# Where TensorE's operands lie in a partition: one place for all streamed tiles of a two-block model

## The chip, the cores and the metric

The kernel runs on one core of a Trainium2 chip. The metric is the device time of one execution in microseconds. A partition of SBUF is addressed in bytes; "place" below means an address in the partition modulo 256.

## The reference, cut to what matters

A token matrix `x` (256 tokens, 1,024 features, float32) goes through two layers of a first block and one layer of a second.

```python
for l in range(2):
    x = x + 0.5 * swiglu(rms_norm(x), gate, up, down)        # 1024 -> 2816 -> 1024
    proj = rms_norm(x) @ w_in                                 # 1024 -> 2944
    x = x + concat(rwkv7(proj), dilated_attention(proj), conv(proj)) @ w_out
    x = x + 0.5 * swiglu(rms_norm(x), gate, up, down)
h  = modulate(rms_norm(x));  hc = modulate(rms_norm(ctx))
ya, ys, yc = window_attention(h, hc), ssm(h, hc), grid_attention(h, hc)
x = x + gate1 * ((ga * (ya @ w_oa) + gb * (ys @ w_ob) + gc * (yc @ w_oc)) @ w_out)
h2 = modulate(rms_norm(x))
x = x + gate2 * ((silu(dwconv(h2 @ w_gate)) * (h2 @ w_up)) @ w_down)
return rms_norm(x) * final_norm
```

## The kernel before

Features lie on partitions, tokens along the partition, so a dense layer is a sum of products of 128 by 128 weight tiles (the stationary operand) with 128 by 256 activation tiles (the moving operand). To keep float32 accuracy every factor is split into a high part, rounded to the type `fp32r`, and a low part, the rest. `dense` then does three matmuls for one weight tile: high weights with high activations, low weights with high activations, high weights with low activations. Each matmul carries its own weight load, which runs beside the matmul before it.

Weights stream from HBM in chunks of eight tiles (`load_chunk`): SyncE's queue loads `wraw`, ScalarE writes `whi` (line 288 is the helper `act`), VectorE writes `wlo` (line 264 is the helper `tt`, line 283 `stt`), three buffers of each. All matmuls are recorded under line 291 (`mm`), transposes under line 295. The names of the stages in the trace are: `gu` gate and up projections of a feed-forward, `dn` its down projection, `win` the input projection of a first-block layer, `woa` and `wob` the two parts of its output projection, `c` and `p` the projections of context and tokens in the second block, `oa`, `ob`, `oc` the three branch projections, `o` the product with `w_out` in the second block (and, 64 rows of it, attention). The scheduler of the tile framework orders instructions on each engine by its own model of time; pinned instructions keep the program's order.

Activation tiles live in these tiles of SBUF:

- `xm`, a ring of 18 slots from `xt()`: the split `x` of every `gu`, `win`, `p` stage, and the inputs of `ob`, `o` and of the last feed-forward.
- `bigA`, `bigB` (6,144 columns each): the split hidden activations of a feed-forward (22 tiles of 256), the moving operands of `dn`; between feed-forwards they are working space.
- `F`: the split context, moving operand of `c`.
- `mixr` and `xr`, one ring: moving operands of `wob`, `oa` and `oc`.
- `E`, one working arena of 10,944 columns, from which `E(offset, shape)` cuts pieces.

The last feed-forward (`ffn_conv`) is different in two ways: its moving tile has 258 columns (two columns carry the shift), and in its down projection `down` the activations are the stationary operand (128 columns of `hh` or `hl`) while the weights move (512 columns of `whi` or `wlo`, 264 matmuls).

Tiles follow each other in the order of their first allocation, each rounded up to 32 bytes. Worked out from the tile sizes:

| tile | place before | place after |
|---|---|---|
| `whi`, `wlo` (every 128-column weight slice) | 32 | 32 |
| `xm` slots | 32, 64, 96, ... (1,056 bytes apart, all eight multiples of 32) | 224 (1,024 bytes apart) |
| `bigA`, `bigB` | 96 | 224 |
| `E`, or `Ea` and `Eb` | 96 | 224 |
| `F` | 128 | 224 |
| `mixr`, `xr` | 224 | 224 |

The distance of a moving operand behind the weights (its place less the weights' place, modulo 256) is therefore before: 64 in `dn`, 96 in `c`, 192 in `wob`, `oa` and `oc`, and any multiple of 32 in the stages that read `xm`. In the last down projection, with the roles changed (weights move, activations are stationary), it is 192 before.

Of the kernel before, what the change touches and what calls it, by code (L numbers as in the profile page):

```python
# [12 lines left out]
F32R = mybir.dt.float32r  # L13
# [7 lines left out]
P = 128  # L21
TOK = 256
# [4 lines left out]
XM = 18  # L27
XR = 8
BIG = 6144
EXT = 10944  # L30
FXT = 4096
# [177 lines left out]
class Ker:  # L209
# [16 lines left out]

    def arena(self, n, tag="E"):

        t = self.t([P, n], tag)

        def piece(off, *shape):
            m = 1
            for z in shape:
                m *= z
            a = t[:, off:off + m]
            if len(shape) == 1:
                return a
            nm = " ".join(f"d{i}" for i in range(len(shape)))
            return a.rearrange(f"p ({nm}) -> p {nm}", **{f"d{i}": z for i, z in enumerate(shape) if i})
        return piece  # L240

    def pin(self, ins):
        return self.tc.keep_in_program_order(ins)

    def xt(self, n=TOK):
        return self.t([P, TOK + 2], "xm", bufs=XM, dt=F32R)[:, 0:n]

# [223 lines left out]
    def setup(self):  # L471
# [30 lines left out]
        self.act(self.ones_r, t0.to_broadcast([P, P]), AF.Identity, bias=1.0)  # L502
        self.norm_begin()
        self.xs = [self.prep(k, g0[:, k:k + 1], False) for k in range(KD)]
        with self.first(-LATE):
# [3 lines left out]
    def load_b(self, name, parts, extra=None):  # L509
        idx, a = _cat(parts)  # L510
        t = self.t([P, 2180], "cb")
        n = a.shape[1]
        self.pin(self.nc.sync.dma_start(out=t[:, :n], in_=self.A[name]))
        if extra:
            idx["lora"] = (n, n + 384)
            self.pin(self.nc.sync.dma_start(out=t[:, n:n + 384], in_=self.A[extra]))
        return lambda k: t[:, idx[k][0]:idx[k][1]]
# [13 lines left out]
    def ffn(self, l, w, nxt):  # L531
# [3 lines left out]
        hh = self.t([P, BIG], "bigA", dt=F32R)  # L535
        hl = self.t([P, BIG], "bigB", dt=F32R)
        E = self.arena(EXT)
        mods = self.mod_part(E, 2 * l + w - 1)
# [40 lines left out]
    def mixer1(self, l, nxt):  # L579
        nc = self.nc  # L580
        col = lambda k, a=0, n=1: self.col(f"{k}.{l}", a, n)
        cb = self.load_b("cb1", _const_b1(), f"lora{l}")
        xs = self.xs
        R1, R2, E, F = self.arena(BIG, "bigA"), self.arena(BIG, "bigB"), self.arena(EXT), self.arena(FXT, "F")
        pb = R2(0, 10, TOK + 2)
        nc.gpsimd.memset(pb[:, :, 0:1], 0.0)
        mum = self.t([P, 10], "mum")
        self.ts(mum, col("shift_mu", 0, 10), -1.0, 1.0)
        att = E(8640, 9, TOK)
        cu = E(6016, 4, TOK)  # L590
        ps_sh = [R2(2600, 3, TOK), R1(0, 3, TOK), E(1536, 3, TOK)]
# [396 lines left out]
    def conv(self, l, cb, col, cu, E):  # L988
        nc = self.nc
        W = 30 + TOK  # L990
        z = E(7040, 2, W)
        nc.gpsimd.memset(z[:, :, 0:30], 0.0)
        th = E(7616, 2, TOK)
        self.act(th, cu[:, 2:4, :], AF.Tanh, scale=0.5)
        self.stt(z[:, :, 30:W], th, 1.0, cu[:, 0:2, :], ALU.add, ALU.mult)
        wh = self.t([P, 62], "cwh")
        self.ts(wh, col("conv_dw_w", 0, 62), 0.5, None)
        o = E(8128, 2, TOK)
        yield

        for j in range(31):
            for i in range(2):
                a, w = z[:, i, j:j + TOK], wh[:, i * 31 + j:i * 31 + j + 1]
# [9 lines left out]
        for i in range(2):  # L1013
            self.stt(o[:, i, :], ps[:, 0:TOK], -1.0 / 256, o[:, i, :])
        sq = E(7616, 2, TOK)
        self.act(sq, o, AF.Square)
# [202 lines left out]
    def ctx_path(self):  # L1219
        nc = self.nc  # L1220
        E, xs, R1 = self.E2, self.cxs, self.R1
# [5 lines left out]
        self.ts(self.cwh[:, 36:48], self.col("ssm_conv_b_2", 0, 12), 0.5, None)  # L1227
        pre = E(5120, 10, TOK + 2)
        nc.gpsimd.memset(pre[:, :, 0:1], 0.0)
# [87 lines left out]
    def block2(self):  # L1317
# [108 lines left out]
        self.norm_begin()  # L1426
        ys = []
        for i in range(KD):
            ps = self.pa("yT")
# [4 lines left out]
            self.norm_add(v)  # L1434
            hi = self.xt()
            lo = self.xt()
            g = self.col("ssm_norm_2", i)
# [11 lines left out]
        for n in range(KD):  # L1449
# [12 lines left out]
            ms.append((hi, lo))  # L1462
        self.norm_begin()
        for n in range(KD):
            if n == 0:
# [8 lines left out]

            xh, xl = self.xt(TOK + 2), self.xt(TOK + 2)
            sh = self.mod[:, 24 + n:26 + n]
# [204 lines left out]
    def ffn_conv(self):  # L1681
        nc = self.nc
        gp = nc.gpsimd
        xs = self.xs
        hh = self.t([P, BIG], "bigA", dt=F32R)
        hl = self.t([P, BIG], "bigB", dt=F32R)
        E = self.arena(EXT)
        rb = None
# [5 lines left out]
        self.add(wh[:, 88:110], wh[:, 88:110], w3[:, :, 2])  # L1694
        fg = E(9216, 1024)
        nc.sync.dma_start(out=fg, in_=self.A["fnorm"])
        pre = E(128, 3, 258)

        self.g2 = E(4096, 1024)
        self.wring = self.t([P, FXT], "F")  # L1700
# [8 lines left out]
        for n in range(NF):  # L1709
# [5 lines left out]
            pr = pre[:, n % 3]  # L1715
            o = E(1024 + (n % 2) * 1024, TOK)
            th = E(1024 + (n % 2) * 1024 + 256, TOK)
            u = E(1024 + (n % 2) * 1024 + 512, TOK)

            sc = E(3072 + (n % 2) * 4, 4)  # L1720
            self.act(sc[:, 0:1], pg[:, TOK:TOK + 1])
# [33 lines left out]
        down((NF - 2, NF - 1), (0, 1))  # L1755
        o = E(5120, 2, 1024)
        rs = []
        for tt in range(2):
            ss = self.t([P, 2], "fss", bufs=2)
            sq = E(7168, 512)  # L1760
            for q in range(2):
# [136 lines left out]
```

## Time and profile before

| | |
|---|---|
| time, median of 3 runs | 1751.85 us (1749.54 to 1753.95) |
| the profiled execution's own time | 1752.03 us |
| its span, first to last instruction | 1750.2 us |
| TensorE matmul (PE) busy | 1709.0 us, 98% |
| TensorE weight load (PEld) busy | 1622.7 us, 93% |
| VectorE (DVE) busy | 1368.0 us, 78% |
| ScalarE (ACT) busy | 942.8 us, 54% |
| GpSimd (POOL) busy | 481.6 us, 28% |

A matmul record is 0.28 us long for 256 columns, but matmuls overlap in the pipeline; what one costs is the distance from its start to the next start. In a group of n back-to-back matmuls that is the group's busy time less the 0.28 us of the last record, divided by n - 1.

### The profile page before, as it was taken

The page shows a single profiled execution, that of the slowest core. Times are in us where ns is not written, and L with a number is a line of the kernel's source. Part 1 is how long each engine was busy: PE and PEld are TensorE (multiplying, and loading weights), DVE is VectorE, ACT ScalarE, POOL GpSimd, SP SyncE. Part 2 cuts the span into 40 slices and gives each one's busy share as a digit, 9 for nine tenths or more (in the row PEclk, how much of TensorE's full clock was granted, in tenths as well). Part 3 has the DMA queues.
Part 4 walks back from the last instruction along what each step waited for, and adds up shares of the span by engine and source line. Part 5 has one row for each costly group of instructions (what it writes and reads, how often), then busy time and mean ns, then how long its engine had stood idle before and what let it go on. Part 6 is the DMA issues. An engine that isn't in the chain of part 4 may idle for free.

```text
span 1750.2 us, 34287 instructions
## 1 busy us (share of the span) xinstructions
PE 1709.0 (98%) x13614; PEld 1622.7 (93%) x13614; DVE 1368.0 (78%) x2436; ACT 942.8 (54%) x1735; POOL 481.6 (28%) x425
## 2 busy tenths in 40 slices
PE   8999999999999999999999999999999999999997
PEld 8999997889999999999888999998998889999976
DVE  7885689858885778668886888877887876789887
ACT  5544476436444544447644545455766665466633
POOL 2221128302220122112830222033751040122143
PEclk9999998999999999999899999999999999999999
DMA  6665542016665577554101678553433225555533
GB/s 233 242 239 183 207 154 73 1 61 216 242 218 191 194 280 280 192 206 163 66 9 63 214 289 279 190 181 123 158 132 109 80 78 192 171 192 188 175 121 120
DMA packets 82128, 293.42 MB, mean 168 GB/s; under 512 B 9008, under 2 KB 10800, under 8 KB 81968
## 3 DMA queue, kind: packets, MB, share of 16 engines
q1 hardware_dynamic: 81968, 291.24, 48.0%
q8 instruction: 106, 1.74, 0.4%
q14 instruction: 54, 0.44, 0.1%
HBM read 290.15 MB, written 1.05 MB: 166 GB/s over the span
## 4 chain that ended last, share of the span: by engine, by line
PE 82%; DVE 10%; ACT 3%; issue 2%; POOL 2%; DMA 1%; SPq 0%; DVEq 0%; ACTq 0%; POOLq 0%
PE gu L291 33%; PE dn L291 17%; PE p L291 7%; PE win L291 5%; DVE wlo L264 3%; PE o L291 2%; PE l L291 2%; PE lt L291 1%; DVE E L283 1%; PE woa L291 1%; PE sc L291 1%; PE ob L291 1%; ACT whi L288 1%; POOL E L264 1%; PE s L291 1%
## 5 line engine op out<-in xcount | busy, mean ns | idle before, releaser
L288 ACT ACTIVATE whi<-wraw 128x1024 fp32r<-128x1024 f32 (+2 forms) x485 | 495.3, 1025 | 506.8 <-issue 188.9
L264 DVE TENSOR_TENSOR wlo<-wraw,whi 128x1024 fp32r<-128x1024 f32 (+2 forms) x477 | 574.2, 1204 | 197.2 <-ACT whi L288 189.0
L291 PE MATMUL gu<-xm,whi 128*128 128x256 f32 (+1 forms) x3520 | 633.3, 283 | 6.5 <-ACT whi L288 4.5
L291 PEld LDWEIGHTS gu<-xm,whi 128*128 128x128 f32 x3520 | 545.1, 190 | 8.3 <-ACT whi L288 4.7
L291 PE MATMUL gu<-xm,wlo 128*128 128x256 f32 (+1 forms) x1760 | 496.0, 282 | 2.6 <-DVE wlo L264 2.5
L291 PEld LDWEIGHTS gu<-xm,wlo 128*128 128x128 f32 x1760 | 334.3, 190 | 4.5 <-DVE wlo L264 4.5
L264 POOL TENSOR_TENSOR bigB<-E,bigA 128x256 fp32r<-128x256 f32 x110 | 144.2, 1314 | 560.6 <-ACT bigA L288 535.2
L291 PE MATMUL dn<-bigB,whi 128*128 128x256 f32 x704 | 196.5, 280 | 0.0
L291 PE MATMUL dn<-bigA,wlo 128*128 128x256 f32 x704 | 196.1, 279 | 0.0
L291 PE MATMUL dn<-bigA,whi 128*128 128x256 f32 x704 | 195.9, 279 | 0.0
L291 PE MATMUL p<-xm,whi 128*128 128x256 f32 x912 | 179.4, 290 | 1.8 <-DVE bigB L283 1.8
L291 PEld LDWEIGHTS p<-xm,whi 128*128 128x128 f32 x912 | 145.2, 190 | 8.3 <-issue 7.1
L264 POOL TENSOR_TENSOR E<-E 128x256 f32<-128x256 f32 x130 | 113.2, 897 | 104.7 <-ACT E L288 103.4
L291 PE MATMUL win<-xm,whi 128*128 128x256 f32 x736 | 139.7, 289 | 0.0
L291 PEld LDWEIGHTS dn<-bigB,whi 128*128 128x128 f32 x704 | 132.1, 188 | 0.0
L291 PEld LDWEIGHTS dn<-bigA,wlo 128*128 128x128 f32 x704 | 132.1, 188 | 0.0
L291 PEld LDWEIGHTS dn<-bigA,whi 128*128 128x128 f32 x704 | 131.5, 187 | 0.0
L291 PE MATMUL p<-xm,wlo 128*128 128x256 f32 x456 | 130.5, 286 | 0.0
L291 PEld LDWEIGHTS win<-xm,whi 128*128 128x128 f32 x736 | 116.2, 193 | 3.9 <-issue 3.9
L291 PE MATMUL win<-xm,wlo 128*128 128x256 f32 x368 | 105.5, 288 | 0.0
L264 DVE TENSOR_TENSOR E<-gu,rb 128x512 f32<-128x512 f32 (+1 forms) x136 | 78.3, 585 | 28.6 <-PE gu L291 28.4
L288 ACT ACTIVATE E<-E 128x256 f32<-128x256 f32 (+3 forms) x196 | 74.7, 404 | 29.1 <-DVE E L264 10.2
(471 smaller groups left out, 2937.6 us busy)
## 6 DMA issues: line engine op xcount, KB each, us to landing
wraw<-in_wflat_dram SPq DMA_DIRECT2D x464, 512.0 KB, 3.6
E<-in_wmod_dram SPq DMA_DIRECT2D x48, 512.0 KB, 4.8
F<-in_wflat_dram SPq DMA_DIRECT2D x22, 512.0 KB, 4.4
E<-in_cc_dram SPq DMA_DIRECT2D x6, 512.0 KB, 6.2
cb<-in_cb_dram SPq DMA_DIRECT2D x2, 832.0 KB, 5.4
E<-in_ctxT_dram SPq DMA_DIRECT2D x1, 1024.0 KB, 6.1
out_dram<-E SPq DMA_DIRECT2D x4, 256.0 KB, 2.1
x<-in_xT_dram SPq DMA_DIRECT2D x3, 256.0 KB, 5.6
```

What stands on the lines that cost most here:

```text
L264: (eng or self.nc.vector).tensor_tensor(out=out, in0=a, in1=b, op=op)
L283: self.nc.vector.scalar_tensor_tensor(out=out, in0=a, scalar=s, in1=b, op0=op0, op1=op1)
L288: self.nc.scalar.activation(out=out, in_=a, func=func, **kw)
L291: return self.nc.tensor.matmul(out, l, r, start=start, stop=stop, skip_group_check=True)
```

## The change

All streamed activation tiles are moved to place 224, 192 bytes behind the weights' place. An unused tile of 48 columns (`gap`) is allocated before `xm`, whose slots shrink from 258 to 256 columns; `cb` shrinks from 2,180 to 2,048 columns; a second unused tile (`gap2`, 40 columns) behind `F` keeps what follows where it was. The 258-column tiles of the last feed-forward no longer fit `xm`; they become pieces, 384 columns apart, of a tile `gx` in `bigA`. The inputs of `ob` become a tile `yp` in `bigA` too. The working arena is two tiles, `Ea` (6,144 columns) and `Eb` (4,992 columns), and pieces move so that none crosses the border. In the last feed-forward `hh` moves from `bigA` to `Ea`, its small pieces are packed closer in `Eb`, and the output tile lies in `bigA`. The context's `pre` moves from `E` to `bigB`. No instruction of computation is added or removed. In the last down projection the stationary operands lie at 224 and the moving weights at 32, so the distance there becomes 64.

```diff
-EXT = 10944
+EXT, EXA = 11136, 6144
+XW = 384
+GAP, GAP2 = 48, 40
...
+    def arena2(self):
+        a, b = self.arena(EXA, "Ea"), self.arena(EXT - EXA, "Eb")
+        return lambda off, *shape: a(off, *shape) if off < EXA else b(off - EXA, *shape)
...
-    def xt(self, n=TOK):
-        return self.t([P, TOK + 2], "xm", bufs=XM, dt=F32R)[:, 0:n]
+    def xt(self):
+        return self.t([P, TOK], "xm", bufs=XM, dt=F32R)
...
         self.norm_begin()
+
+        self.t([P, GAP], "gap")
         self.xs = [self.prep(k, g0[:, k:k + 1], False) for k in range(KD)]
...
-        t = self.t([P, 2180], "cb")
+        t = self.t([P, 2048], "cb")
...
-        E = self.arena(EXT)
+        E = self.arena2()
         mods = self.mod_part(E, 2 * l + w - 1)
...
-        R1, R2, E, F = self.arena(BIG, "bigA"), self.arena(BIG, "bigB"), self.arena(EXT), self.arena(FXT, "F")
+        R1, R2, E, F = self.arena(BIG, "bigA"), self.arena(BIG, "bigB"), self.arena2(), self.arena(FXT, "F")
         pb = R2(0, 10, TOK + 2)
         nc.gpsimd.memset(pb[:, :, 0:1], 0.0)
+        if l == 0:
+            self.t([P, GAP2], "gap2")
...
-        att = E(8640, 9, TOK)
-        cu = E(6016, 4, TOK)
+        att = E(8832, 9, TOK)
+        cu = E(6144, 4, TOK)
...
-        pre = E(5120, 10, TOK + 2)
+        pre = self.R2(0, 10, TOK + 2)
...
+        yp = self.t([P, BIG], "bigA", dt=F32R)
         for i in range(KD):
...
-            hi = self.xt()
-            lo = self.xt()
+            hi, lo = (yp[:, (2 * i + a) * TOK:(2 * i + a + 1) * TOK] for a in range(2))
...
+        gx = self.t([P, BIG], "bigA", dt=F32R)
...
-            xh, xl = self.xt(TOK + 2), self.xt(TOK + 2)
+            xh, xl = (gx[:, (2 * n + z) * XW:(2 * n + z) * XW + TOK + 2] for z in range(2))
...
-        hh = self.t([P, BIG], "bigA", dt=F32R)
+        hh = self.t([P, EXA], "Ea", dt=F32R)
         hl = self.t([P, BIG], "bigB", dt=F32R)
-        E = self.arena(EXT)
+        E = self.arena(EXT - EXA, "Eb")
...
-        o = E(5120, 2, 1024)
+        A = self.arena(BIG, "bigA")
+        o = A(0, 2, 1024)
...
-            sq = E(7168, 512)
+            sq = A(2048, 512)
```

The lines left out move further pieces of the arena by a constant.

## Rows read from the trace of the kernel before

**Rows 1.** The page: busy time of the matmul engine, granted clock in 40 slices.

```profile
PE 1709.0 (98%) x13614; PEld 1622.7 (93%) x13614; DVE 1368.0 (78%) x2436; ACT 942.8 (54%) x1735; POOL 481.6 (28%) x425
...
PEclk9999998999999999999899999999999999999999
```

**Rows 2.** The page: chain that ended last, by engine and by line.

```profile
PE 82%; DVE 10%; ACT 3%; issue 2%; POOL 2%; DMA 1%; SPq 0%; DVEq 0%; ACTq 0%; POOLq 0%
PE gu L291 33%; PE dn L291 17%; PE p L291 7%; PE win L291 5%; DVE wlo L264 3%; PE o L291 2%; PE l L291 2%; PE lt L291 1%; DVE E L283 1%; PE woa L291 1%; PE sc L291 1%; PE ob L291 1%; ACT whi L288 1%; POOL E L264 1%; PE s L291 1%
```

**Rows 3.** Windows, wob alone: window, its length, PE busy us (matmuls), clock, DMA.

```profile
385.00:395.00 10.00, 8.34 (x72) 1.00 0.33 113
953.00:963.00 10.00, 8.35 (x72) 1.00 0.38 122
```

**Rows 4.** Windows, dn alone: first and last of the four stages.

```profile
137.00:201.00 64.00, 62.36 (x528) 1.00 0.57 200
...
1089.50:1153.00 63.50, 62.14 (x528) 1.00 0.59 202
```

**Rows 5.** Windows, gu alone: third stage, and the last feed-forward.

```profile
583.00:709.00 126.00, 125.07 (x1056) 1.00 0.72 255
...
1543.00:1673.00 130.00, 127.71 (x1056) 1.00 0.50 169
```

**Rows 6.** Windows, one tile each: oa, then ob, then o.

```profile
1493.00:1498.70 5.70, 5.66 (x48) 1.00 0.59 201
...
1498.00:1522.00 24.00, 22.85 (x192) 1.00 0.55 178
...
1521.00:1545.00 24.00, 23.08 (x192) 1.00 0.54 178
```

**Rows 7.** Chain that ended last, in order: start us, us, what.

```profile
47.06 90.81 PE gu L291 x767
...
206.92 21.54 PE win L291 x184
...
1467.24 5.65 PE p L291 x48
```

**Rows 8.** Timeline of PE in wob: start us, us, instructions.

```profile
953.80 0.28 PE L291 MATMUL wob<-mixr,wlo 128*128 128x256 f32 x1
...
954.38 0.50 PE L291 MATMUL wob<-mixr,whi 128*128 128x256 f32 x3
...
956.08 0.39 PE L291 MATMUL wob<-mixr,whi 128*128 128x256 f32 x2
```

**Rows 9.** Timeline of PE in c, five weight tiles apart.

```profile
1155.18 0.40 PE L291 MATMUL c<-F,whi 128*128 128x256 f32 x2
...
1156.98 0.40 PE L291 MATMUL c<-F,whi 128*128 128x256 f32 x2
```

**Rows 10.** Windows, all engines: length, PE, PEld, DVE, ACT, POOL busy, clock, DMA.

```profile
386.50:394.00 7.50, 7.50 (x69) 7.50 (x68) 5.90 (x11) 5.28 (x11) 2.02 (x2) 1.00 0.41 142
...
592.00:708.00 116.00, 116.00 (x985) 116.00 (x984) 95.34 (x129) 57.71 (x84) 29.81 (x21) 1.00 0.74 263
...
1550.00:1660.00 110.00, 110.00 (x917) 110.00 (x917) 98.87 (x182) 68.96 (x174) 19.12 (x18) 1.00 0.53 180
```

**Rows 11.** Waits between 1550 and 1660 us: total us, times, longest.

```profile
ACT whi L288 <- PE gu L291: 31.6, 31, 1.3
```

**Rows 12.** Chain that ended last between 1660 and 1692 us.

```profile
1669.04 1.68 DVE F L334
...
1681.56 2.35 POOL F L334
...
1685.03 3.00 DVE wlo L264
```

**Rows 13.** Timeline of PE in the last down projection, six matmuls apart.

```profile
1713.79 0.40 PE L291 MATMUL dn<-wlo,bigA 128*128 128x512 f32 x1
...
1715.19 0.40 PE L291 MATMUL dn<-wlo,bigA 128*128 128x512 f32 x1
```

More of the change, by code (lines that the diff above doesn't have):

```diff
@@ L225, in t, with arena @@
         return self.sb.tile(shape, dt, tag=tag, bufs=bufs, name=name or tag)
-    def arena(self, n, tag="E"):
+    def arena(self, n, tag):
         t = self.t([P, n], tag)
@@ L990, in conv @@
         W = 30 + TOK
-        z = E(7040, 2, W)
+        z = E(7168, 2, W)
         nc.gpsimd.memset(z[:, :, 0:30], 0.0)
-        th = E(7616, 2, TOK)
+        th = E(7744, 2, TOK)
         self.act(th, cu[:, 2:4, :], AF.Tanh, scale=0.5)
@@ L997, in conv @@
         self.ts(wh, col("conv_dw_w", 0, 62), 0.5, None)
-        o = E(8128, 2, TOK)
+        o = E(8256, 2, TOK)
         yield
@@ L1014, in conv @@
             self.stt(o[:, i, :], ps[:, 0:TOK], -1.0 / 256, o[:, i, :])
-        sq = E(7616, 2, TOK)
+        sq = E(7744, 2, TOK)
         self.act(sq, o, AF.Square)
@@ L1694, in ffn_conv @@
         self.add(wh[:, 88:110], wh[:, 88:110], w3[:, :, 2])
-        fg = E(9216, 1024)
+        fg = E(3472, 1024)
         nc.sync.dma_start(out=fg, in_=self.A["fnorm"])
-        pre = E(128, 3, 258)
-        self.g2 = E(4096, 1024)
+        pre = E(112, 3, 258)
+        self.g2 = E(2448, 1024)
         self.wring = self.t([P, FXT], "F")
@@ L1715, in ffn_conv @@
             pr = pre[:, n % 3]
[L1716 to L1720, printed above, removed]
+            o, th, u = (E(896 + (n % 2) * 768 + z * TOK, TOK) for z in range(3))
+            sc = E(2432 + (n % 2) * 4, 4)
             self.act(sc[:, 0:1], pg[:, TOK:TOK + 1])
```

## The prediction

> **What bounds the kernel now.** I read the page first: the matmul engine is busy 98% of the span, at a granted clock of full speed (2.4 GHz) in nearly all slices [rows 1]. The reader should see that little idle time is left to win; what is left is the price of one matmul. The chain that ended last says where that price counts: PE holds 82% of it, and the long split-float32 stages `gu`, `dn`, `p`, `win`, `o` hold most of that [rows 2]. So a change of the time per matmul in these stages goes to the end of the kernel nearly one for one, and elsewhere hardly.
>
> Next I read windows with one tile name alone, which give the pace of a stage: busy time less the last record's 0.28 us, over the number of steps. All of these stages do the same thing (three matmuls of 256 columns for each weight tile), yet the pace differs. `wob`: (8.34 - 0.28) / 71 = 113.5 ns, and 113.7 in the other layer [rows 3]. `dn`: (62.36 - 0.28) / 527 = 117.8 ns, the last of the four 117.4 [rows 4]. `gu`: (125.07 - 0.28) / 1055 = 118.3 ns, in the last feed-forward, with 258 columns, 120.8 [rows 5]. `ob` 118.2, `o` 119.4, while `oa` has 114.5 with a short stall at its start in it [rows 6]. `c` takes 1.80 us for 15 matmuls where nothing stops it, 120.0 ns [rows 9].
>
> Put beside the places of the operands, the pattern is: where every moving operand lies 192 behind the weights (`wob`, `oa`), 113.5; where all lie 64 behind (`dn`), 117.8; where all lie 96 behind (`c`), 120.0; where they are mixed (`gu`, `ob`, `o`), 118 to 121. `wob` and `oa` lie in different stages and blocks, and share only this place.
>
> **The change, part by part.** The move of `xm`, `bigA`, `bigB` and `F` brings every dense stage to the distance of `wob`. I take its pace, 113.6 ns, for all, and 0.8 ns more where 258 columns are streamed (two columns at the 2.4 GHz of the clock's row). Stages that follow PE alone (PE busy through the whole window, [rows 10]):
>
> - `gu`, four feed-forwards: the first runs freely from 47.06 us, 767 matmuls in 90.81 us, 118.4 each [rows 7]: 767 x 4.8 ns = 3.7 us. The other three: 3 x 1056 x 4.7 ns = 14.9 us. Together 18.6.
> - `dn`: three times 528 x 4.2 ns = 6.7, the last 528 x 3.8 = 2.0. Together 8.7.
> - last feed-forward's `gu`: 120.8 - 114.4 = 6.4 ns x 1056 = 6.8.
> - `ob` 192 x 4.6 = 0.9, `o` 192 x 5.8 = 1.1. Together 2.0.
> - `win` until attention and the recurrence begin, 540 of its 1104 matmuls at 117.1 (21.54 us for 184, [rows 7]): 540 x 3.5 = 1.9.
> - `p` ahead of `oa`, 246 of its 1368 matmuls at 117.7 (5.65 us for 48, [rows 7]): 1.0.
>
> The sum is 39.0 us.
>
> Stages where PE shares the path with chains of VectorE, ScalarE and GpSimd: `c` 360 x 6.4 = 2.3, the other 1122 of `p` x 4.1 = 4.6, the other 564 of `win` x 3.5 = 2.0, `woa` 240 x 4 = 1.0; 9.9 us, of which anything from nothing to all counts. PE's 82% of the chain as a mean is too kind here, since the 18% of the others sit in just these stages; I take half, 5.0.
>
> The last feed-forward gives back some. VectorE is busy 98.87 of 110 us there, 90% [rows 10]; with PE 5.3% quicker it would need 95%. ScalarE's weight splits still wait for PE there, 31.6 us in all [rows 11], so VectorE's 11 us of idle time are waits that shrink with PE. But from 1660 us on the chain runs through VectorE and GpSimd (gating of the last weights, the late `wlo` splits, 3.00 us for the last [rows 12]), and PE arrives there earlier while they have as much to do. Of the 6.8 us between none and all is lost; I take half, 3.4.
>
> The last down projection keeps 264 matmuls of 512 columns at 1.40 us for six, 233 ns [rows 13], now at distance 64 and not 192. The trace has no 512-column run at 64. One weight load falls on one matmul as in the other stages, so the bounds are the spread of the 256-column paces: 120.0 - 113.5 = 6.5 ns either way, 264 x 6.5 = 1.7 us. I take nothing, since 512 columns at the present 192 are no quicker than two halves (2 x 113.6 = 227).
>
> Edits at no cost: the two unused tiles hold only space. `arena2`, `yp`, `gx` and the moved `pre` change which earlier readers a first write waits for. `yp` waits for the last reader of `bigA` (second attention, over long before), while before it waited for slots of `xm` still read by the last `p`; `gx` waits for `ob`, which `o` follows in any case; `pre`'s memset on GpSimd waits for the last `dn`, and what is queued behind it on GpSimd is work on `c`'s outputs, which come after. `fg`'s load on SyncE's queue waits for `Eb` alone where it waited for all of `E`, so the weight loads queued behind it are no later. `hh` in `Ea` waits for readers of `z`, done before `oa` ends. What covers `yp`'s writes is `oa` itself, 96 matmuls or 10.9 us of PE work between them and `ob`; without that cover they would show as a wait of PE ahead of `ob`. For slots that come free sooner I count nothing.
>
> The sum: 39.0 + 5.0 - 3.4 = 40.6 us off the profiled execution's 1752.0 gives 1711.4; that execution is 0.2 us above the median of the runs, so I forecast **1711 us**. Bounds of this case: all shared stages and the 512-column bound in favour and no loss at the end, 39.0 + 9.9 + 1.7 = 50.6, 1701; none of the shared, all of the loss, the bound against, 39.0 - 6.8 - 1.7 = 30.5, 1722.
>
> The paces of `wob` and `dn` differ by 4.2 ns, with the same instructions and the same clock [rows 3, 4]. The Trainium skill speaks against reading this as a matter of place: "TensorE: Matmul & The Clock Gate", in "Step-by-step: what each phase is for", says that TensorE has two independent SBUF read ports, one for the streamed operand and one for the weights, so that loading the next tile's weights takes no read bandwidth from the running matmul. By that rule the distance changes nothing and the sum is 0, not 40.6. The trace does not agree with it as far as the paces go, and the rule is a rival below.
>
> **The rivals.** *The place sets the pace only in short runs.* `wob` begins with five steps of 116 ns (0.58 us) and then holds 113.3 (1.70 us for 15) [rows 8]; if long runs, under more DMA traffic (263 against 142 GB/s, [rows 10]), fall back to 116 half of the time or more, about half of the gain stays: 1752 - 20 = 1732. Against it: `dn` holds one pace in four long runs [rows 4]. Chance 0.14.
>
> *The place does nothing.* `wob` and `oa` would be quicker for something else that they share, such as being short. For it: the mixed stages, with moving operands at eight distances, are about as quick as `dn` with one. Then only the order of instructions moves: 1747 to 1756. Against it: `oa` and `wob` stand in different blocks with other work around them. Chance 0.09. This is where the page of the Trainium skill named above would lead.
>
> *One place is no gain in itself, and the long runs go to `c`'s pace.* `c` too has all its moving operands at one distance, in a long run, and is at 120.0 ns the slowest of the 256-column stages [rows 9]. If 113.5 belongs to short runs and 120.0 to long ones, `gu` gains 1.7 ns x 3935 = 6.7 us, `dn` 2.2 x 2112 = 4.6, `win`, `p`, `ob` about 2.2 x 978 = 2.2, half of the shared stages 2: 1752 + 15.5 = 1767.5. It decides for slower from a pace of 118.3 in `gu` upwards. Against it: `dn`, as long, is at 117.8 and steady. Chance 0.07.
>
> **How the numbers follow.** The forecast case has a chance of 0.70, with its own range 1701 to 1722; it is far above the others because three separate stages at 192 agree and four at 64 agree. Nine tenths of it and more lie inside 1702 to 1732, which also takes in about half of the half-gain case; with it the range holds 0.8. A measurement of this kernel tells 0.3%, 5.3 us, from no change. Faster by more than that are the first two cases and a little of the third, 0.86; within it most of the third, 0.07; slower the fourth, 0.07.
>
> **What would show it.** Right: windows of `dn` alone with some 60.2 us for 528 matmuls, `gu` some 120.2 for 1056 (third feed-forward), `c` steps of 113 to 114, the clock unchanged, VectorE's busy time unchanged and its share up. The last `dn` at 233 ns, with the gap ahead of it a few us wider. Wrong: `dn` still at 117 or more (place does nothing), `gu` between 115 and 117 (half), or new waits of PE at the start of `o`, at the last feed-forward's start, or on VectorE in its middle that eat what the pace gives.

## The result, and the profile after

The changed kernel takes 1730.99 us in the median of four runs (1728.84 to 1741.27), beside 1750.69 us (1748.04 to 1753.95) for the kernel before on the same chip: a ratio of 0.9891, 95% interval 0.9849 to 0.9932. A fifth execution on record took 1726.52 us. The change makes the kernel faster by 19.7 us, and the forecast was 40.6. The time lies inside the range, but less than half of the forecast gain came.

The profiled execution is the longest of the four: 1741.27 us, span 1739.5 us; the other three have spans of 1727.1 to 1729.5 us. So a second profile of the same kernel (run `e15_again`, below) is read beside it, with 1730.41 us and a span of 1728.6 us. Line numbers are 8 higher than before in both (`mm` is line 299, `act` 296, `tt` 272).

The page of the changed kernel, busy time and granted clock, as in [rows 1]:

```profile
PE 1695.5 (97%) x13614; PEld 1609.4 (93%) x13614; DVE 1369.7 (79%) x2436; ACT 942.8 (54%) x1735; POOL 477.2 (27%) x425
...
PEclk9999998999999999999999999999999999999999
```

Same number of matmuls, same clock, VectorE as busy as before (1369.7 against 1368.0 us). PE has 13.5 us less. Windows of the changed kernel with `gu` alone (window, its length, PE busy us (matmuls), PEld, VectorE, ScalarE, clock, DMA share, GB/s), the four feed-forwards and then the last one:

```profile
3.90:138.00 134.10, 130.31 (x1056) 127.78 (x1056) 14.46 (x23) 0.00 (x0) 1.00 0.69 238
395.50:522.40 126.90, 125.33 (x1056) 124.57 (x1056) 14.34 (x22) 0.00 (x0) 1.00 0.65 228
584.00:705.00 121.00, 120.35 (x1056) 120.17 (x1056) 14.62 (x23) 0.00 (x0) 1.00 0.75 266
952.00:1081.00 129.00, 126.94 (x1056) 126.16 (x1056) 14.37 (x22) 0.00 (x0) 0.99 0.74 259
1532.00:1662.00 130.00, 128.24 (x1056) 127.78 (x1056) 17.16 (x42) 6.54 (x43) 1.00 0.49 170
```

The same view with `dn` alone, the four feed-forwards:

```profile
137.00:200.00 63.00, 62.33 (x528) 62.26 (x528) 2.94 (x7) 0.00 (x0) 1.00 0.56 199
522.00:585.00 63.00, 62.35 (x528) 62.26 (x528) 3.29 (x8) 0.00 (x0) 1.00 0.54 185
704.00:765.00 61.00, 60.00 (x528) 59.91 (x528) 3.27 (x8) 0.00 (x0) 1.00 0.59 208
1080.00:1142.00 62.00, 60.72 (x528) 60.54 (x528) 3.11 (x8) 0.00 (x0) 1.00 0.60 208
```

Here is the surprise. The third `gu` has 120.35 us where 120.2 was forecast, the third `dn` 60.00 where 60.2 was. But the second `gu` and `dn` stand at 125.33 and 62.35, about as in [rows 4, 5]: same instructions, same places, same clock, and if anything less DMA traffic (228 against 266 GB/s). `dn` has 113.3 ns for one matmul in the third stage, (60.00 - 0.28) / 527, and 117.8 in the second, and the trace has hardly a value between: rows of hundreds of matmuls at 113.33 and rows of hundreds at 117.78. I call them the quick and the slow pace; a group of three takes 340 ns in the one and 353.3 in the other.

Where one turns into the other is seen in the timeline of PE. In the third `gu` of the changed kernel, every third matmul (the one with `wlo`) and a single matmul of another job (`nb`, a broadcast with the weights `ones`, which lie at place 128):

```profile
590.57 0.28 PE L299 MATMUL gu<-xm,wlo 128*128 128x256 f32 x1
590.92 0.28 PE L299 MATMUL gu<-xm,wlo 128*128 128x256 f32 x1
...
591.16 0.28 PE L299 MATMUL nb<-xm,ones 128*128 128x256 f32 x1
...
591.74 0.28 PE L299 MATMUL gu<-xm,wlo 128*128 128x256 f32 x1
592.08 0.28 PE L299 MATMUL gu<-xm,wlo 128*128 128x256 f32 x1
```

Three matmuls take 0.35 us ahead of `nb` and 0.34 behind it, and 0.34 stays until the stage ends, with `dn` behind it. In the second `gu` it goes the other way, and no other job is in between; one matmul is late (its record is 0.32 us long):

```profile
406.10 0.28 PE L299 MATMUL gu<-xm,wlo 128*128 128x256 f32 x1
406.44 0.32 PE L299 MATMUL gu<-xm,wlo 128*128 128x256 f32 x1
...
407.19 0.28 PE L299 MATMUL gu<-xm,wlo 128*128 128x256 f32 x1
407.54 0.28 PE L299 MATMUL gu<-xm,wlo 128*128 128x256 f32 x1
```

From there 0.35 us holds to 591 us, through the whole `dn`. So a pace, once taken, stays until something disturbs the row.

### The profile page after: what moved, and what is told of

Same layout as the page of the kernel before. It is cut to its first block, busy times and chain, and to the rows that moved or that the text cites. A ratio compares the mean times of both kernels' runs of the same rounds, so it can differ in the third digit from the quotient of the medians.

```text
span 1739.5 us, 34265 instructions
## 1 busy us (share of the span) xinstructions
PE 1695.5 (97%) x13614; PEld 1609.4 (93%) x13614; DVE 1369.7 (79%) x2436; ACT 942.8 (54%) x1735; POOL 477.2 (27%) x425
## 4 chain that ended last, share of the span: by engine, by line
PE 80%; DVE 12%; POOL 3%; issue 2%; ACT 2%; DMA 1%; SPq 0%; DVEq 0%; ACTq 0%; POOLq 0%
PE gu L299 33%; PE dn L299 16%; PE p L299 7%; PE win L299 5%; DVE wlo L272 4%; PE o L299 2%; PE l L299 2%; PE lt L299 1%; PE woa L299 1%; DVE Eb L291 1%; PE ob L299 1%; POOL Eb L272 1%; DVE bigA L272 1%; ACT whi L296 1%; PE s L299 1%
## 5 line engine op out<-in xcount | busy, mean ns | idle before, releaser
L299 PE MATMUL gu<-xm,whi 128*128 128x256 f32 x2816 | 499.3, 282 | 7.3 <-ACT whi L296 4.8
L299 PEld LDWEIGHTS gu<-xm,whi 128*128 128x128 f32 x2816 | 434.4, 191 | 8.7 <-ACT whi L296 5.0
L299 PE MATMUL gu<-xm,wlo 128*128 128x256 f32 x1408 | 396.3, 282 | 2.9 <-DVE wlo L272 2.9
L299 PEld LDWEIGHTS gu<-xm,wlo 128*128 128x128 f32 x1408 | 266.3, 189 | 5.0 <-DVE wlo L272 4.8
L272 POOL TENSOR_TENSOR bigB<-Ea,bigA 128x256 fp32r<-128x256 f32 x88 | 121.9, 1388 | 438.8 <-ACT bigA L296 438.8
L272 POOL TENSOR_TENSOR Eb<-Eb 128x256 f32<-128x256 f32 x120 | 105.6, 906 | 100.6 <-ACT Eb L296 100.2
L299 PE MATMUL gu<-bigA,whi 128*128 128x258 f32 x704 | 128.1, 284 | 0.0
L299 PEld LDWEIGHTS win<-xm,whi 128*128 128x128 f32 x736 | 115.9, 193 | 3.6 <-issue 3.6
L299 PEld LDWEIGHTS gu<-bigA,whi 128*128 128x128 f32 x704 | 109.8, 191 | 0.0
```

Source lines behind the costliest of these rows:

```text
L272: (eng or self.nc.vector).tensor_tensor(out=out, in0=a, in1=b, op=op)
L299: return self.nc.tensor.matmul(out, l, r, start=start, stop=stop, skip_group_check=True)
```

## The experiments

All ran beside the kernel before, whose median in the five sets was 1750.25 to 1750.93 us.

**e1_again**: the changed kernel, unchanged, one more profile.

> The changed kernel once more, as it is. Theory 'two paces': with all operands at one place PE's matmuls settle into one of two exact paces, 113.3 or 117.8 ns, and every stop or foreign matmul draws anew; then stages change sides against the first profile (there dn was slow, slow, fast, fast and the second and fourth gu slow, the third fast), and the time lies anywhere between 1722 and 1742. Rival 'traffic': the pace follows the DMA and VectorE load of a stage; then the same stages are fast and slow as in the first profile, to within 0.5 us each.

Measured, in one run: 1722.3 us, span 1720.5. The first and third `gu` are quick, the second slow until its end; `dn` is quick but for the second (60.00, 62.35, 60.00, 60.26 us busy). It is not bound to a stage which pace it takes: in the first `gu` and `dn` the two profiles differ. But the third `gu` is quick in both, and the second turns slow at the same matmul (more on this below).

**e2_d64, e3_d0**: all moving operands but those of `wob`, `oa` and `oc` (they stay at 192) at one other distance, by the two unused tiles alone; tiles, pieces and instructions are those of the changed kernel.

```diff
-GAP, GAP2 = 48, 40
+GAP, GAP2 = 16, 72        # distance 64;  64, 24 for distance 0
```

> All streamed tiles 64 behind the weights instead of 192 (the unused tile in front has 16 columns, the one behind F 72); mixr and xr stay at 192. Theory 'two paces', one place is enough: both paces appear again in dn and gu, time 1722 to 1745. Rival 'the distance 192 counts': dn and gu at 117.8 throughout as dn was before, only wob, oa, oc fast, time 1747 to 1752.

> All streamed tiles at the weights' own place (distance 0; unused tiles of 64 and 24 columns). Two paces: both appear, perhaps in other shares, 1720 to 1745. 'The distance counts': one pace, unlike 113.3, in all stages; if streams at the same place disturb each other most, 120 or more, 1760 or above.

Measured: distance 64 gives 1748.17 us, ratio 0.999 (0.9975 to 1.0004), distance 0 gives 1766.43 us, 1.0099 (1.0074 to 1.0125). Windows of the third `dn`, first of the kernel with 64:

```profile
707.00:770.00 63.00, 62.35 (x528) 62.26 (x528) 3.12 (x8) 0.00 (x0) 1.00 0.61 200
```

then of the kernel with 0:

```profile
715.00:779.50 64.50, 63.52 (x528) 63.43 (x528) 3.37 (x8) 0.00 (x0) 1.00 0.60 197
```

(62.35 - 0.28) / 527 = 117.8 ns and 120.0 ns; both kernels hold one pace in all `gu` and `dn` stages (but for 36 matmuls). The place alone moves the kernel over 35 us, from 1766 to 1731. By the rule of the Trainium skill that the prediction weighed ("TensorE: Matmul & The Clock Gate", "Step-by-step: what each phase is for": loading the next weights takes no read bandwidth from the running matmul), as the prediction read it, these kernels would be equal; they are not. The weights lie at place 32 in every run, though, so the runs show the effect of the moving operand's place and not whether it is its distance from the weights that counts; "distance" below means no more than that. And distance 64, in the rivals' words "one place", gains nothing over the mixed places of before.

**e4_oldplaces**: the changed kernel's tiles (`gx`, `yp`, two arenas, `hh` in `Ea`) with the places of before (but for `gx` and `yp`, which lie in `bigA` and so at distance 64).

```diff
-GAP, GAP2 = 48, 40
+GAP2 = 8
-EXT, EXA = 11136, 6144
+EXT, EXA = 11072, 6144
...
-        return self.t([P, TOK], "xm", bufs=XM, dt=F32R)
+        return self.t([P, TOK + 2], "xm", bufs=XM, dt=F32R)[:, 0:TOK]
...
-        self.t([P, GAP], "gap")
...
-        att = E(8832, 9, TOK)
+        att = E(8768, 9, TOK)
```

> The changed kernel's tiles (two arenas, ob's and the last feed-forward's operands in bigA, hh in Ea) with the places of before: xm slots 1,056 bytes apart, bigA, bigB and F 64 behind the weights. If the places alone make the gain, gu, win and p go back to 118 and the time is 1746 to 1752. Rival 'the tiles': what is won comes from fewer waits for xm slots and arena, and the time stays under 1740 with gu at 118.

Measured: 1747.99 us, ratio 0.9992 (0.9977 to 1.0006). Windows of this kernel, the third `gu`:

```profile
584.00:710.00 126.00, 125.07 (x1056) 124.89 (x1056) 14.81 (x23) 0.00 (x0) 1.00 0.74 256
```

125.07 us, to the hundredth what [rows 5] show. The new tiles by themselves are worth nothing that these runs can tell from zero; the places make the gain.

**e5_d224, e6_d160, e7_d128, e8_d32**: the other distances, by the same line (`GAP, GAP2` = 56, 32; 40, 48; 32, 56; 8, 80).

> All streamed tiles 224 behind the weights (unused tiles of 56 and 32 columns). So far: at 0 one pace of 120.0 ns, at 64 one of 117.8, at 192 two, 113.3 and 117.8. If the fast pace belongs to a stretch of distances around 192, it is here too and the time is 1720 to 1745; if 192 alone has it, one pace of 117.8 or 120 and 1748 to 1767.

> The same at distance 160 (40 and 48 columns). A stretch of distances: both paces or the fast one alone, 1705 to 1745 (1705 if the fast one is the only one). 192 alone: 1748 to 1767.

> The same at distance 128 (32 and 56 columns), half the period away from the pace of 120.0 at distance 0. If disturbance falls steadily with the distance from 0, 128 is the best: 113.3 or less throughout and 1705 or less. If not: 117 to 120 and 1745 to 1767.

> The same at distance 32 (8 and 80 columns), between 0 (120.0) and 64 (117.8): steady between them, 118 to 120 and 1750 to 1766; if distances act in no order, anything from 113.3 to 122.

Measured, with the pace of the third `gu` and `dn` worked out from their windows, (busy - 0.28) / (n - 1):

| distance | time, us | ratio (interval) | `gu`, ns | `dn`, ns | 258-column `gu`, busy us |
|---|---|---|---|---|---|
| 0 | 1766.43 | 1.0099 (1.0074 to 1.0125) | 120.2 | 120.0 | 127.41 |
| 32 | 1741.77 | 0.9954 (0.9936 to 0.9971) | 116.9 | 116.7 | 127.36 |
| 64 | 1748.17 | 0.999 (0.9975 to 1.0004) | 118.0 | 117.8 | 126.13 |
| 128 | 1759.0 | 1.0047 (1.0031 to 1.0063) | 118.9 | 118.7 | 129.70 |
| 160 | 1750.72 | 1.0005 (0.999 to 1.002) | 117.6 | 117.3 | 127.37 |
| 192 (the change) | 1730.99 | 0.9891 (0.9849 to 0.9932) | 113.8 | 113.3 or 117.8 | 128.24 |
| 224 | 1752.98 | 1.0019 (1.0003 to 1.0035) | 118.6 | 118.3 | 127.37 |

With the 120.0 of `c` at 96 [rows 9], the mean of the eight `gu` paces is (120.2 + 116.9 + 118.0 + 120.0 + 118.9 + 117.6 + 113.8 + 118.6) / 8 = 118.0 ns; the mixed places of before had 118.3 [rows 5]. So the mixed stages had about what a mean over places makes, and this answers what had spoken for "the place does nothing". The paces follow no order in the distance: 128, farthest from 0, has 118.7 and 32 has 116.7. Only 192 has the quick pace over whole stages. At 64 it was seen in long rows only at one spot: in the last `dn` of before the first 102 matmuls take 11.57 us, 113.4 each, and the rest 117.8 (the same in e4; the change comes at two `nb`); so 64 may have the same two paces and nearly always be in the slow one (e16 below).

**e9_fine**: places between the multiples of 32, in the four `dn` alone, and the 258-column tile `gx` at distance 64.

```diff
+        b = (4, 60, 2, 62)[2 * l + w - 1]
...
-            sl = slice(n * TOK, (n + 1) * TOK)
+            sl = slice(b + n * TOK, b + (n + 1) * TOK)
```

> The changed kernel with the moving tiles of the four down projections at four other distances behind the weights, in steps smaller than 32 bytes: 208, 176, 200 and 184 (in the order of the stages), and the last feed-forward's input tile at distance 64. Theory (the paces go with 32-byte lines, 192 to 223 is one line): dn at 208 and 200 shows the two paces of 192, 113.3 or 117.8 ns, and at 176 and 184 the pace of 160, 117.7 to 118.0. Rival (each distance has a pace of its own): at least one of the four is outside 113.3 to 118, or 200 and 208 lie apart from 192. Both: the last feed-forward's gu goes from 120.8 to 118.7 ns (as in the run with the old places), 2.2 us less. Time by either between 1720 and 1745 us.

Measured: 1742.41 us. Windows of `dn` alone, the first at distance 208 and the last at 184:

```profile
132.90:197.00 64.10, 63.09 (x528) 62.98 (x528) 3.37 (x8) 0.00 (x0) 1.00 0.59 199
...
1079.20:1144.50 65.30, 63.77 (x528) 63.57 (x528) 3.36 (x8) 0.00 (x0) 1.00 0.58 196
```

119.2 and 120.5 ns; between them 176 with 63.12 us, 119.2, and 200 with 63.52, 120.0. The theory of 32-byte lines fell: 208 and 200 have nothing of 192, and all four are slower than every multiple of 32 but 0 and 96 (120.0 each). Eight bytes beside 192 its pace is gone.

**e10_kick, e11_kick_same**: single matmuls put between weight tiles. Their results go into halves of PSUM tiles that nothing reads or that are overwritten, so they add work and change no value. In e10 their weights are `ones` (place 128), in e11 a tile of the current chunk (place 32, as in the stage itself). There are 34 of them and not the 33 of the text: `ob` has two.

```diff
+    def kick(self, out, x):
+        self.pin(self.mm(out, self.ones_r, x, True, True))      # e11: self.cur[2][:, 0:P]
...
+                if n in (2, 4, 8):                               # gu
+                    self.kick(ps[:, TOK:512], xs[0][0])
...
+            if n in (0, 1, 3):                                   # dn
+                self.kick(ps[:, TOK:512], hs[0][0])
...
+            if j in (2, 4, 6):                                   # win
+                self.kick(ps[:, TOK:512], xs[0][0])
```

> The changed kernel with 33 single foreign matmuls (weights: the ones, at place 128; result into halves of PSUM tiles that nothing reads) put between weight tiles: three in each gu and each dn stage, three in each win, one in ob, two in o. Theory (two paces at distance 192, chosen anew at each break of the row; a foreign matmul with weights at 128 mostly leaves PE in the quick one): at most a third of the slow steps of the 256-column stages is left, 4,600 x 2/3 x 4.4 ns = 13.6 us less, the 33 matmuls cost 3.8 us, so 1731 - 10 = 1721 us (1714 to 1727), and the slow stretches end at the inserted matmuls. Rival (the slow pace belongs to a stage and its load, not to the last break): slow stretches go on across the inserted matmuls, 1731 + 4 = 1735 us or more. Rival (the chance of the quick pace is the same at each break, about as often as in the two looks): as many slow steps as before, in more and shorter stretches, 1725 to 1740 us.

> The same 33 inserted matmuls, but with weights of the current chunk (place 32, distance 192 as all others) instead of the ones (place 128). Theory (it is the other place of the foreign weights that resets the pace): a matmul more with the same places changes nothing, long slow stretches stay, 1730 to 1745 us. Rival (any matmul that breaks the row of three does it): as quick as the kernel with the ones, 1714 to 1727 us.

Measured: e10 1733.21 us, ratio 0.9904 (0.9883 to 0.9925); e11 1744.44 us, 0.9968 (0.9954 to 0.9982). Timeline of e10 in the first `gu`, which was in the slow pace there (`wlo` matmuls and the inserted one):

```profile
54.75 0.28 PE L299 MATMUL gu<-xm,wlo 128*128 128x256 f32 x1
55.10 0.28 PE L299 MATMUL gu<-xm,wlo 128*128 128x256 f32 x1
...
55.69 0.29 PE L299 MATMUL gu<-xm,ones 128*128 128x256 f32 x1
...
56.65 0.28 PE L299 MATMUL gu<-xm,wlo 128*128 128x256 f32 x1
56.99 0.28 PE L299 MATMUL gu<-xm,wlo 128*128 128x256 f32 x1
```

And of e11 in the second `gu`, where the inserted matmul makes a group of three with `whi`:

```profile
411.50 0.28 PE L299 MATMUL gu<-xm,wlo 128*128 128x256 f32 x1
411.85 0.28 PE L299 MATMUL gu<-xm,wlo 128*128 128x256 f32 x1
411.97 0.52 PE L299 MATMUL gu<-xm,whi 128*128 128x256 f32 x3
412.32 0.28 PE L299 MATMUL gu<-xm,wlo 128*128 128x256 f32 x1
412.67 0.28 PE L299 MATMUL gu<-xm,wlo 128*128 128x256 f32 x1
```

0.35 becomes 0.34 in e10 and stays 0.35 in e11. Over the whole of e10, 25 of the 34 inserted matmuls met the quick pace and left it so; 6 met the slow pace, and all 6 turned it quick within some six steps; 2 stood in a broken row. One is an exception: it stood right behind two `nb`, which have the same weights, in a row that had been quick, and the row was slow behind the three. In e11 the slow pace runs through nine of them, from 398 to 583 us and from 960 to 1075 us. So an additional matmul alone does not reset the pace; one with the weights `ones` does.

Then why is e10 no quicker than the changed kernel? Its `gu` and `dn` are (120.48 and 60.37 us in the third stages, all inserted matmuls included). The timeline shows a new wait, ahead of the last 256-column `dn`:

```profile
1061.89 0.28 PE L299 MATMUL gu<-xm,whi 128*128 128x256 f32 x1
1069.09 1.04 PE L299 MATMUL nb<-xm,ones 128*128 128x256 f32 x2 [6.92 <-ACT xm L296]
```

and the window behind it the lower clock, 25 matmuls in 5.3 us:

```profile
1069.50:1074.80 5.30, 5.30 (x25) 5.25 (x25) 4.32 (x12) 0.00 (x0) 0.00 (x0) 0.50 0.01 3
```

An inserted matmul is pinned behind all that the program has recorded before it, and it drew an `nb`, which waits for ScalarE, ahead of `dn`. PE stood idle 6.9 us, and went on at a granted clock of 0.50, the lower level of 1.2 GHz. Without it the start of `dn` comes 7.9 us sooner, and `dn` itself takes some 2.4 us less. e11 has the same wait.

**e12_kick_gx**: e10 with `gx` at distance 64 (offset 32 columns).

> The kernel with the 33 foreign matmuls, and the last feed-forward's input tile moved by 32 columns, to distance 64. Theory: 258 columns take 118.7 ns at 64 and 120.8 at 192, 1,056 x 2.1 ns = 2.2 us less than the kernel with the matmuls alone, about 1719 us, quicker than both kernels. Rival (VectorE and GpSimd at the end of the last feed-forward take the gain back): equal within 1 us.

Measured: 1734.74 us (1731.54 to 1737.06), ratio 0.9913 (0.9892 to 0.9934), not to be told from e10. The 258-column `gu` is 1.9 us shorter, as in e14 below.

**e13_kick2, e14_kick_gx2, e15_again**: the inserted matmuls without the wait (26: two in each `dn`, from the third output tile on in the last one; one in each `win`), the same with `gx` at distance 64, and the changed kernel as it is, on one chip.

```diff
-            if n in (0, 1, 3):
+            if n in ((2, 4) if nxt is None else (0, 3)):
...
-            if j in (2, 4, 6):
+            if j == 4:
```

> The changed kernel with 26 foreign matmuls (weights: the ones, at place 128; results go into halves of PSUM tiles that nothing reads): as in the kernel with the inserted matmuls, but two in each dn, later in the last of them, so that no waiting matmul is pulled ahead of it, and one in each win. Theory (the slow pace of long rows is where the gain went): the stall of 7.2 us and the low clock behind it, some 5 us, are gone, gu and dn stay at 113.3 to 113.6 ns: 1733 - 12 - 2 = 1719 us (1714 to 1723). Rival (what is won in pace is lost elsewhere): 1727 us or more with gu and dn at the quick pace.

> The same 26 foreign matmuls, and the last feed-forward's input tile at distance 64 (258 columns at 119.0 instead of 120.8 ns, 1,056 x 1.8 ns = 1.9 us). Theory: 1717 us, 1.9 us under the kernel without this move. Rival (the end of the last feed-forward gives it back): equal within 0.7 us.

> The changed kernel, unchanged. Theory (which pace a long row takes differs from run to run): a wide spread, 1722 to 1745 us, a wider one than that of the kernel with the inserted matmuls, and a median near 1731 us. Rival (it is the same in every run of one program): a spread within 0.3%, 5 us.

Measured: e13 1722.87 us (1719.03 to 1724.63), ratio 0.9841 (0.9825 to 0.9857); e14 1722.05 us (1720.04 to 1723.55), 0.9839 (0.9824 to 0.9854); e15 1730.02 us (1729.13 to 1733.99), 0.989 (0.9873 to 0.9908). Windows of e13, the second and third `gu`:

```profile
388.00:511.50 123.50, 121.44 (x1059) 120.65 (x1059) 14.40 (x23) 0.00 (x0) 1.00 0.68 235
570.90:692.00 121.10, 120.48 (x1059) 120.23 (x1059) 15.00 (x23) 0.00 (x0) 1.00 0.75 266
```

and of e15, the first and second `gu`:

```profile
3.90:134.00 130.10, 126.19 (x1056) 123.84 (x1056) 14.75 (x23) 0.00 (x0) 1.00 0.73 245
386.90:514.00 127.10, 125.33 (x1056) 124.52 (x1056) 14.36 (x22) 0.00 (x0) 1.00 0.67 228
```

With the quick pace held, 26 matmuls more make the kernel 7 us quicker; no run of e13 or e14 is as long as the shortest of e15. It beats both kernels. `gx` at 64 takes 1.9 us from the last `gu` (126.35 against 128.24 us busy), but the times of e13 and e14 can't be told apart. The spread that was expected of e15 did not come: its four runs lie within 5 us, while all executions of the changed kernel on record go from 1722.30 to 1741.27 us. The choice still differs between profiles (the first `gu` was slow in the first profile and quick in the other two), so what picks it is neither fixed nor wholly free.

**e16_kick64, e17_kick_p224, e18_kick_p96**: the 26 inserted matmuls again. e16 has all moving operands at distance 64 (`GAP, GAP2 = 16, 72`). e17 and e18 are e13 with other weights in the inserted matmuls, 128 columns of their own moving tile, at place 224 and at 96.

```diff
-        self.pin(self.mm(out, self.ones_r, x, True, True))
+        self.pin(self.mm(out, x[:, 0:P], x, True, True))       # e17, place 224; e18: x[:, 32:32 + P], place 96
```

> All moving operands at distance 64, and the 26 foreign matmuls (weights: the ones, at place 128; results read by nothing) as in the quickest kernel. Theory (64 has the same two paces as 192, and only the disturbance decides): gu and dn go to 113.3 ns behind the inserted matmuls, 1720 to 1728 us. Rival (at 64 a disturbance leads back to the slow pace): gu and dn stay at 117.8, 1748 + 3 = 1745 to 1753 us.

> The changed kernel with the 26 inserted matmuls, their weights 128 columns of the moving tile itself, at place 224 (distance 0) instead of the ones at 128. Theory (any foreign place of the weights brings the quick pace): 1720 to 1726 us, slow rows end at the inserted matmuls. Rival (place 128 is special, or the ones are): slow rows go on across them, or quick rows turn slow there, 1730 us or more.

> As the one before, with weights at place 96 (distance 128). Theory (any foreign place): 1720 to 1726 us. Rival (place 128 is special, or the ones are): 1730 us or more, with slow rows across the inserted matmuls.

Measured: e16 1749.81 us, ratio 1.0002 (0.999 to 1.0015); e17 1749.98 us, 1.0006 (0.9996 to 1.0017); e18 1725.46 us (1719.08 to 1734.14), 0.9872 (0.9833 to 0.9911). Timeline of e17 in the third `gu`, which came in quick; the inserted matmul is the one without a weight tile's name:

```profile
594.41 0.28 PE L299 MATMUL gu<-xm,wlo 128*128 128x256 f32 x1
594.75 0.28 PE L299 MATMUL gu<-xm,wlo 128*128 128x256 f32 x1
594.98 0.28 PE L299 MATMUL gu<-xm 128*128 128x256 f32 x1
...
595.57 0.28 PE L299 MATMUL gu<-xm,wlo 128*128 128x256 f32 x1
595.92 0.28 PE L299 MATMUL gu<-xm,wlo 128*128 128x256 f32 x1
```

0.34 becomes 0.35: this matmul makes the row slow. All 5 rows that came to one of them at the quick pace left it at the slow pace, and the 20 that came at the slow pace kept it (the one left of the 26 stands in a broken row), and the kernel is as slow as before the change, 27 us over e13, which has the same instructions on the same tiles but for the weights of 26 matmuls. Which pace the long rows have is thus worth the whole gain of the change and more. In e18 each of them leaves the pace as it is, 17 quick and 8 slow (one more stands ahead of a broken row), and the time spreads over 15 us. So neither theory holds as it stood: a single foreign matmul leaves the row quick with weights at 128, slow with weights at 224, and as it was with weights at 96 and 32. That the place does it is shown for 224 against 96, two pieces of one tile; at 128 only the tile `ones` was tried, so there the place and the tile are not told apart. In e16 no row at distance 64 turned quick behind weights at 128: the two paces that 64 may have can't be chosen in this way.

## Why the prediction was wrong

Gains by part in us, from busy times in windows and the spans; "rest" is what the span gives besides.

| part | forecast | first profile | e15 | e13 |
|---|---|---|---|---|
| four `gu` | 18.6 | 6.4 | 12.1 | 20.1 |
| four `dn` | 8.7 | 3.8 | 6.2 | 7.7 |
| `ob`, `o` | 2.0 | 0.8 | 1.6 | 1.1 |
| last `gu`, less the loss behind it | 3.4 | -0.5 | -0.5 | -0.5 |
| rest (`win`, `p`, `c`, `woa`) | 7.9 | 0.2 | 2.2 | 1.8 |
| span | 40.6 | 10.7 | 21.6 | 30.2 |

**The step that failed first**: "I take its pace, 113.6 ns, for all". The mechanism was right: e2 to e8 show that the place of the moving operands sets the pace, e4 that nothing else in the change makes the gain, and e13, where the quick pace is held, gains 27.8 us in `gu` and `dn` where 27.3 were forecast. What was not seen is that distance 192 has two paces, 113.3 and 117.8 ns, and that a long row can stay at the second; held there, as in e17, the change gains nothing. Short rows such as `wob` and `oa` had mostly shown the first, but not always: the first row of `oa` in the trace of before, ahead of the window that the prediction read, is at the slow pace, and the next at the quick one (0.35 and 0.34 us for three):

```profile
1486.50 0.28 PE L291 MATMUL oa<-xr,wlo 128*128 128x256 f32 x1
1486.85 0.28 PE L291 MATMUL oa<-xr,wlo 128*128 128x256 f32 x1
...
1488.58 0.28 PE L291 MATMUL oa<-xr,wlo 128*128 128x256 f32 x1
1488.92 0.28 PE L291 MATMUL oa<-xr,wlo 128*128 128x256 f32 x1
```

In the profile e15, the typical one, this costs 29.3 - 19.9 = 9.4 us in `gu`, `dn`, `ob` and `o`, half of the 19.0 us that are missing there; 3.9 are the last `gu`, 5.7 the rest. The 27.8 us of e13 flatter the forecast a little: before, 15 matmuls at the start of the fourth `gu` ran at the lower clock, some 1.4 us, and in e13 none did.

**What turns the rows slow.** The late matmul of the second `gu` is no accident. It is the first to use a chunk of `wlo` that VectorE has only just written. VectorE's instruction, and the weight load of that matmul, in the first profile:

```profile
405.10 1.23 DVE L272 TENSOR_TENSOR wlo<-wraw,whi 128x1024 fp32r<-128x1024 f32 x1 [1.48 <-ACT whi L296]
...
406.38 0.19 PEld L299 LDWEIGHTS gu<-xm,wlo 128*128 128x128 f32 x1
```

VectorE ends at 406.33 us, and the load can start only then, 0.06 us ahead of its matmul where others have 0.11. At distance 64 (e2) PE comes to this matmul later after VectorE, 0.19 us instead of 0.12, and nothing waits. The same matmul is late in the second `gu` and its counterpart in the fourth in all eleven profiles of kernels at distance 192, 22 times: 20 times the next matmul starts 159 or 160 ns after it instead of 113, and the row is slow behind it; twice (the fourth `gu` of e1 and of e14) it starts 163 ns after it, and the row is quick again within some six steps. So the quick pace itself brings PE up to a weight split, and the short wait there takes the pace away. The prediction had no wait of this kind.

**The nearest rival** was "the place sets the pace only in short runs", with 1732 us, and the time came about 1 us from it. The range holds the measured time only because its upper end was drawn to take in half of this rival; the forecast case itself ended at 1722, so that is luck and not the forecast's merit. Nor did the rival's reasons hold. Neither length nor traffic decides: the third `gu`, with the heaviest traffic, is quick for 1,000 matmuls, and there is no 116 but a mean of two paces.

**Last feed-forward.** The term 6.8 rested on 258 columns behaving as 256 do. They don't: at 192 its `gu` took 128.24 us against 127.71 before [rows 5]; the table gives its best at 64, 126.13. It had been taken to lose half to VectorE at its end; there was nothing to lose. VectorE and the other engines look as in [rows 10]:

```profile
1538.00:1650.00 112.00, 112.00 (x930) 112.00 (x929) 99.25 (x186) 68.25 (x174) 18.87 (x18) 1.00 0.52 180
```

**Shared stages.** 7.9 us were forecast for `win`, `p`, `c` and `woa`, and 0.2 to 2.2 came. Half was too kind: in e13 the inserted matmuls, some 3 us at 0.12 each, lie nearly all in the terms above, so they don't excuse it. Here the rows are broken by other jobs every few matmuls and both paces alternate. For `c` and `p` the trace tells pace and path apart. Their back-to-back steps did get quicker, from a mean of 119.8 to 115.9 ns in `c` and from 118.0 to 115.2 in `p` (before against e15, start to start in the timeline), which over 360 and 1,368 matmuls is some 5 us. But from the end of the last 256-column `dn` to the start of `ob` it took 346.4 us before, 346.2 in e15 and 345.3 in e1. So the path was wrong here: PE's steps went quicker and the stretch hardly got shorter. Of 1.0 + 3.5 us that were forecast for it, 0.2 to 1.0 came; which waits took the rest back was not traced.

**Last down projection**, costed at nothing. Timeline of PE in it, in the first profile:

```profile
1700.58 0.39 PE L299 MATMUL dn<-wlo,Ea 128*128 128x512 f32 x1
...
1701.49 0.39 PE L299 MATMUL dn<-wlo,Ea 128*128 128x512 f32 x1
```

Four matmuls in 0.91 us, 228 ns, where [rows 13] had 233; in e15 233 again. It stays inside the bound of 1.7 us, and the chain shows that it wouldn't reach the end: at 228 ns PE waits for the last weights.

```profile
1711.43 3.45 DMA F<-in_wflat_dram
1714.95 3.46 POOL F L342
1719.54 3.48 DVE wlo L272
1723.06 6.92 PE dn L299 x29
```

**What was right:** the edits at no cost (e4), the clock (at full speed in nearly all slices) and VectorE's busy time unchanged, and the quick stages to 0.2 us. No new wait at the start of `o` or of the last feed-forward takes the gain.

**What stays open:** what the chip does inside that makes two paces, and why a step of 160 ns leaves a row slow and one of 163 does not. For a single matmul in between, four places of its weights were tried and each had one answer; why these, no run tells. Whether the distance counts or the moving operand's place alone, and whether the period is 256 bytes, was not tested: the weights never moved. What takes the gain back in `c` and `p`, and how the shortfall of `win` and `woa` divides, is open too.

## What to carry to other kernels

Where TensorE is busy nearly all the time, take the pace of each stage from its windows and set it beside the places of both operands: two unused tiles moved this kernel between 1731 and 1766 us. Before a pace of a short stage is carried to a long one, look at single steps in several long rows and ask whether there is one value or two, and what stands ahead of each row. And where other chains share the path, half of a gain can be far too much: here some 5 us of quicker steps in `c` and `p` gave 1 us or less. A quicker engine also reaches its inputs sooner, so look which of them are ready only just in time.

## What the runs showed of the hardware

- One matmul of 256 columns with a weight load of its own costs 113.3 to 120.5 ns at the full clock, by the place of its moving operand (modulo 256; the weights at 32 throughout). Multiples of 32 differ by up to 6.7 ns, and four places between them gave 119.2 to 120.5.
- At distance 192 there are two steady paces, 113.33 and 117.78 ns, for hundreds of matmuls each, and PE keeps the one it is in. A single matmul between with weights at place 128 leaves a quick row behind it (e10: all 6 that came at the slow pace, all 25 that came at the quick one), at 224 a slow one (all 25), at 96 (25) and at 32 (9 in slow rows) the one that was there. A matmul late by some 45 ns turned quick into slow in 20 of 22 cases.
- The best distance for 256 columns isn't the best for 258: 128.24 us at 192 and 126.13 at 64 for the same 1,056 matmuls.
- After 6.9 us without work TensorE went on at a granted clock of 0.50 (1.2 GHz): the next 25 matmuls took 5.3 us.
